# Attention heads of a hybrid decoder layer: the spatial result fetched in turned 32 by 32 blocks and transposed by VectorE instead of TensorE

## The chip, the cores and the metric

The kernel runs on one core of a Trainium2 chip. A core has five engines that run their own queues of instructions: TensorE (PE; its weight loads, which overlap its products, are shown apart as PEld), VectorE (DVE), ScalarE (ACT), GpSimd (POOL) and SyncE (SP), which here issues nearly all transfers. Sixteen DMA engines move data between device memory (HBM) and the on-chip memory SBUF. TensorE writes its results to PSUM, a small memory of eight banks of 128 partitions by 512 floats; the other engines read them there.

The metric is the device time of one launch in microseconds (us). The kernel before takes 1564.72 us, the median of three runs (1563.97 to 1565.47).

## The reference, cut to what matters

One layer with two token mixers, sequence 512, width 2048, sixteen heads and sixteen groups of 128 channels, everything in float32:

```python
proj = h @ w_in[l]
q_lat, kv_lat, k_rope, z_mla, u, v, z_sgu, g_mla, g_sgu = split_cols(proj, IN_SPLITS)
...
y_mla = causal_mla_attention(q_nope, q_rope, k_nope, k_rope, v_mla) * jax.nn.silu(z_mla)
y_sgu = chunked_causal_sgu(u, v, sgu_norm_g[l], w_spatial[l], b_spatial[l]) * jax.nn.silu(z_sgu)
merged = jax.nn.sigmoid(g_mla) * y_mla + jax.nn.sigmoid(g_sgu) * y_sgu
x = x + gate[:, None] * (merged @ w_out[l])
return rmsnorm(x, final_norm_g)
```

What the change touches is the second term of `merged`, sigmoid(g_sgu) * y_sgu, called the spatial result below. For each head (128 channels) it is added to the gated output of the attention.

## The kernel before, in words

Products are made with float32 values split into a high and a low part: three matrix products (`mm3`, lines 148 to 150) for one. The splitting is ScalarE's (a copy to the rounded type, the high part, L118 for weights and L153 for activations) and VectorE's (the difference, the low part, L119 and L136).

The kernel first makes the wide projection, the gates and the spatial result, token blocks by channels, and stores the spatial result in device memory (`t_d`, one tensor for four heads, shape token block x 128 tokens x 512 channels). The gate of the attention's output goes the same way (`gt_d`, for heads 12 to 15 already turned in `g_d`). Then come the sixteen heads, and then the output projection.

In the heads, the merged result is wanted with channels on the partitions and tokens along the row, since it is the left operand of the output projection. The spatial result comes the other way, so it has to be transposed: 128x128 for each of the four token blocks. For head h:

- `scores`: 20 products of the head's queries and keys, one PSUM bank or part of one for each query block; the rotated part of the queries enters by L1560 and L1561.
- `softmax`: VectorE adds the mask and takes the maximum, ScalarE takes the exponentials (L1582), VectorE the reciprocals.
- Meanwhile TensorE makes the queries of head h + 1 (`qproj`), and in even heads also the rotary queries of the next pair (`rproj`).
- `transposes` (L1600): TensorE transposes the exponentials, ScalarE and VectorE split them.
- `kproj`: keys of head h + 1, split by `kfinish` (the row d<-ps,d of L136 on VectorE).
- `turn` (L1626): four TensorE transposes of the gate for heads below 12 (called gated here), and four of the spatial result for all heads.
- `pv`: the product of the transposed exponentials and the values, 12 products into one bank.
- `merge_a`: VectorE multiplies that bank by the gate (sig<-ps,sig, or sig<-ps,g in the last four heads) and adds the transposed spatial result (sig<-sig,ps); the split of the sum is put off to the next head.
- In even heads VectorE then works at two or three pieces of a sum for the output gate (L139); in odd heads it rotates the queries of the next pair (`rfinish`), and TensorE makes the next pair's values (`vproj`).

The program is written in the order in which each engine works; there is no planner in this part. Weights come through `Stream`: a ring of three raw buffers filled by the SP queue (L99) and split by ScalarE and VectorE into a ring of two pairs. The SP queue works in order; a load of weights there waits until VectorE has split the buffer's former contents. `load_before(granule, f)` puts other transfers into that queue just ahead of the load of one granule. The granules of a head are `gq[h]` (queries), `gr[p]` (rotary queries of pair p), `gk[h]` (keys) and `gvv[p]` (values). PSUM banks are handed out in turn from a ring of seven (`bank()`; bank 0 is `rproj`'s).

`fetch(h)` brings the spatial result of a head (tile b, `vt[h]`) and its gate (tile g, `gt[h]`) into SBUF. For heads 1 to 15 it stands ahead of the load of `gk[h]`; head 0's is issued before the first product of the heads.

Of the kernel before, what the change touches and what calls it, by code (L numbers as in the profile page):

```python
# [11 lines left out]
F32 = mybir.dt.float32  # L12
# [8 lines left out]
P = 128  # L21
D = 2048
S = 512
KC = D // P
NB = S // P
# [103 lines left out]
def trunk_layer(ctx, tc, xT, xn, c, vecs, pos, wada, w1, w2, wv, wv3, wv4, wh, wh15, wq, wqr, wk, wvv, wo, wsT, bsp, gfin, out,  # L129
                dbg=None):  # L130
    nc = tc.nc
    ACT, DVE, PE, DMA = nc.scalar, nc.vector, nc.tensor, nc.sync
# [14 lines left out]
    def mm3(ps, ah, al, bh, bl, start, stop):  # L147
        PE.matmul(ps, ah, bh, start=start, stop=False)  # L148
        PE.matmul(ps, ah, bl, start=False, stop=False)  # L149
        PE.matmul(ps, al, bh, start=False, stop=stop)  # L150
# [18 lines left out]
    def nt(p, shape, dt, tag, **kw):  # L169
        uid[0] += 1  # L170
        return p.tile(shape, dt, tag=tag, name=f"{tag}_{uid[0]}", **kw)
# [48 lines left out]
    def scratch(name, shape):  # L220
        return dram.tile(shape, F32, name=name, tag=name)
# [14 lines left out]
    t_d = [scratch(f"t_d{i}", [NB, P, S]) for i in range(4)]  # L236
# [30 lines left out]
    gq, gr, gk, gvv = {}, {}, {}, {}  # L267
# [45 lines left out]
    def get(i, ahead=1, run=1):  # L313
        r = ws.get(i, ahead)
        fs, pend[:] = pend[:run], pend[run:]
        for f in fs:
            f()
        return r
# [8 lines left out]
    def bank_at(k):  # L327
        return nt(psp.p, [P, S], F32, f"ps{k}")

    def bank():  # L330
        n_bank[0] += 1
        return bank_at(ring[(n_bank[0] - 1) % len(ring)])
# [40 lines left out]
    def load_before(granule, f, *a):  # L373
        ws.before.setdefault(granule, []).append(lambda: f(*a))
# [338 lines left out]
    def place(s, us, f, *a):  # L713

        def full(s):
            own, (a, b) = busy.get(s, 0.0) + us, (busy.get(s + d, 0.0) for d in (-1, 1))
            near = [sum(busy.get(s + d + k, 0.0) for k in range(5)) for d in range(-4, 1)]
            return own > 3.3 or own + max(a, b) > 5.75 or s < at_block[T0] + 22 and max(near) + us > 13.4

        while full(s):  # L720
            s += 1
        spend(s, us)
        on(s, BACK, f, *a)
        return s
# [40 lines left out]
    rows = {}  # L765
# [101 lines left out]
    for b in range(1, len(BLOCKS)):  # L867
# [11 lines left out]
        for key in (bl, br_, al, ar):  # L879
            if key[0] == "v":  # L880
                for t in range(2):
                    n, o = 2 * key[2] + t, key[1] * S
# [87 lines left out]
    for g in range(H):  # L970
# [3 lines left out]
        a = s_ + 4  # L974
        on(a, BACK, sgu_scale)
        a = place(a, 0.29, sgu_weights)
        a = place(a, 0.29, sgu_weights_split)
        if g + 1 < H:
            on(a + 1, LOAD, sgu_load, g + 1)
        a = place(max(a, s_ + 5), 0.69, sgu_gain)  # L980
        a = place(a + 1, 0.69, sgu_split)
# [233 lines left out]
    for group in (((10, "lat8"), (11, "lat9")), ((12, "lat10"), ("plain", "sinT"))):  # L1215
# [9 lines left out]
        i = group[0][0]  # L1225
# [124 lines left out]
    bp = tp = None  # L1350
    y_of, z_of = [(1, 2), (0, 7)], (3, 4)
    for b in range(len(BLOCKS)):
        if b == 1:
            ring[:], n_bank[0] = [5, 6], 0
        for g, (p, i) in enumerate(V7):
            s = done[0] = at_block[b] + g
            n = 1 if b or g else 2
# [49 lines left out]
    def at(name, dt, shape=(P, S)):  # L1407
        p, tag = place[name]
        if p is latp.p:
            v = slot(tag, dt)  # L1410
            return v if len(shape) == 2 else v.rearrange("p (n w) -> p n w", n=shape[1])
        return nt(p, list(shape), dt, tag)
# [13 lines left out]
    gt, vt = [None] * H, [None] * H  # L1426
# [34 lines left out]

    def fetch(h):

        vt[h] = nt(bp.p, [P, S], F32, f"b{h}")
        DMA.dma_start(vt[h].rearrange("p (n w) -> p n w", n=NB),
                      t_d[h // 4][:, :, h % 4 * P:(h % 4 + 1) * P].rearrange("n p w -> p n w"))
        gt[h] = nt((ga if h < 8 else g2p).p, [P, S], F32, f"g{h}")
        if h < GATED:
            DMA.dma_start(gt[h].rearrange("p (n w) -> p n w", n=NB),
                          gt_d[h // 4][:, :, h % 4 * P:(h % 4 + 1) * P].rearrange("n p w -> p n w"))  # L1470
        else:
            DMA.dma_start(gt[h], g_d[h - GATED])

    for h in range(1, H):
        load_before(gk[h], fetch, h)


    qt, kt, vv, qs = {}, {}, {}, {}

    def qproj(h, meanwhile=None, then=None):  # L1480
        wH, wL = get(gq[h])
        if meanwhile:
            meanwhile()
        ps = bank()
        for k in range(6):
            sl = slice(k * P, (k + 1) * P)
            mm3(ps, wH[:, sl], wL[:, sl], lh[k], ll[k], k == 0, k == 5)
        if then:
            then()
        qh, ql = at("qh", F32R), at("ql", F32R)  # L1490
        hilo(qh, ql, ps)
        qt[h] = (qh, ql)

    def rproj(p):
        wH, wL = get(gr[p])
        ps = bank_at(0)
        for k in range(6):
            sl = slice(k * P, (k + 1) * P)
            mm3(ps, wH[:, sl], wL[:, sl], lh[k], ll[k], k == 0, k == 5)
        return ps  # L1500
# [12 lines left out]
    def kproj(h):  # L1513
        wH, wL = get(gk[h])
        ps = bank()
        for k in range(4):
            sl = slice(k * P, (k + 1) * P)
            mm3(ps, wH[:, sl], wL[:, sl], lh[6 + k], ll[6 + k], k == 0, k == 3)
        return ps
# [28 lines left out]
    def scores(h):  # L1548
        qh, ql = qt.pop(h)
        kh, kl = kt.pop(h)  # L1550
        q2 = qs.pop(h)
        s3, s2, s1 = bank(), bank(), bank()
        dst = {3: s3, 2: s2[:, :384], 1: s1[:, :256], 0: s1[:, 256:384]}
        for i in (3, 2, 1, 0):
            ps = dst[i]
            n = (i + 1) * P
            q = slice(i * P, (i + 1) * P)
            mm3(ps, qh[:, q], ql[:, q], kh[:, :n], kl[:, :n], True, False)

            PE.matmul(ps, q2[:, q], krh[:, :n], start=False, stop=False)  # L1560
            PE.matmul(ps, q2[:, q], krl[:, :n], start=False, stop=True)  # L1561
        return dst
# [59 lines left out]
    def turn(src):  # L1622
        ps = bank()
        for n in range(NB):
            tk = slice(n * P, (n + 1) * P)
            PE.transpose(ps[:, tk], src[:, tk], ident)  # L1626
        return ps
# [13 lines left out]
    def merge(n=None):  # L1641
        fs, merging[:] = merging[:n], merging[n:] if n else []
        for f in fs:
            f()

    merging = []
    fetch(0)
    rps = rproj(0)
    m2 = at("m2", F32)
    qproj(0, lambda: [f() for f in last_gates], lambda: ws.split_to(gvv[0]))  # L1650
# [7 lines left out]
    def out_granule(cg, i, banks, ahead=1, run=1):  # L1658
        wH, wL = get(go[cg, i], ahead, run)
        for k in range(2):  # L1660
            j = 2 * i + k
            sl = slice(k * 512, (k + 1) * 512)
            for n in range(NB):
                tk = slice(n * P, (n + 1) * P)
                mm3(banks[n], mh[j][:, tk], ml[j][:, tk], wH[:, sl], wL[:, sl], j == 0, j == H - 1)

    for h in range(H):
        if h == H - 1:
            ring[:], n_bank[0] = [4, 5, 6, 7], 0
            ws.split_to(go[0, 0])  # L1670
        dst = scores(h)
        more, odd = h + 1 < H, h % 2 == 1
        pair = h // 2 + 1
        first = go[0, 1] if not more else gr[pair] if not odd and 2 * pair < H else None
        pr_, shares_ = softmax(h, dst, (lambda: ws.split_to(first)) if first is not None else None)
        if more:
            qproj(h + 1, lambda: merge(1 if h == H - 2 else None))
            if not odd and 2 * pair < H:
                rps = rproj(pair)
        else:  # L1680
            pso = [bank_at(k) for k in range(NB)]
            for i in range(2):
                out_granule(0, i, pso)
        pa, fa = transposes(pr_, (0,))
        fa()
        if h < GATED:
            for n in range(NB):
                g_ = gt[h][:, n * P:(n + 1) * P]
                ACT.activation(g_, g_, AF.Copy, scale=shares_[:, n:n + 1])
        pb, fb = transposes(pr_, (1,))  # L1690
        fb()
        pc, fc = transposes(pr_, (2, 3))
        fc()
        if more:
            kps = kproj(h + 1)
            kfinish(h + 1, kps)
        else:
            merge()
            pieces_at(h)
            DVE.tensor_reduce(out=dots[:, 2 * KC:2 * KC + NG], in_=partial, axis=AX.X, op=ALU.add)  # L1700
            gate_sum(0, NG)
            out_granule(0, 2, pso)
            gate_turn(0, NG, bank(), nt(tp, [P, S], F32, "sig", bufs=3))()
        gate_ = gt[h]
        if h < GATED:
            gate_ = nt(tp, [P, S], F32, "sig", bufs=3)
            ACT.copy(gate_, turn(gt[h]))
        tps = turn(vt[h])
        ops = pv(h, {**pa, **pb, **pc})
        merge_a(h, ops, tps, gate_)  # L1710
        if not odd:
            pieces_at(h)
        if not odd and 2 * pair < H:
            m2 = at("m2", F32)
            swapped(m2, rps)
        if more and odd:
            rfinish(pair, rps, m2)
            vproj(pair)
# [36 lines left out]
    rows = []  # L1755
# [39 lines left out]
    for cg in range(3):  # L1795
# [6 lines left out]
        for n in range(NB):  # L1802
            f = lambda n=n, cg=cg, ps=pso[n]: residual(n, cg, slice(cg * 512, (cg + 1) * 512), ps)
# [7 lines left out]
    for n in range(NB):  # L1811
# [16 lines left out]
        y, o = yt[:, n], 1536 + o  # L1828
# [82 lines left out]
```

## Time and profile before

| | |
|---|---|
| median of three runs | 1564.72 us |
| the profiled execution | 1566.76 us, span of its instructions 1565.1 us |
| granted clock of TensorE, mean | 0.999 |
| busy over the span: TensorE, its weight loads, VectorE, ScalarE | 99%, 83%, 78%, 51% |
| DMA | 316.16 MB, 202 GB/s on average |
| heads | from about 1097 to 1400 us |
| L1626 on tile b | 64 transposes, 272 ns each from start to end |
| fetch of tile b | 16 transfers of 256 KB, median 4.9 us from issue to landing |

Times in the profile are microseconds from the start of the span. A row of a group gives line, engine, operation, what is written and read, shape, count, then busy time, mean ns of one, and idle time just before with what ended it. A row of a timeline gives start, duration, engine and work. An engine's idle time costs something only where the end of the kernel depends on it.

### The profile page before, as it was taken

What the parts mean: (1) busy time and instruction counts of PE and PEld (TensorE: products, weight loads), DVE (VectorE), ACT (ScalarE), POOL (GpSimd) and SP (SyncE); (2) the same over time, 40 slices, a digit from 0 to 9 for tenths busy, and PEclk for the clock granted to TensorE, in tenths of its full rate; (3) what the DMA queues carried; (4) which work ended last, traced back from release to release, by engine and by line L of the source; (5) the groups of instructions that cost most, each with busy time, mean ns of one, the idle gap of its engine ahead of it and who ended that gap; (6) DMA issues with size and microseconds to landing.
All of it is one profiled execution on the core that took longest, in us unless ns stands there. A gap on an engine that the chain in (4) does not pass through costs nothing.

```text
span 1565.1 us, 20574 instructions
## 1 busy us (share of the span) xinstructions
PE 1552.7 (99%) x7392; PEld 1296.2 (83%) x7392; DVE 1218.7 (78%) x1667; ACT 802.9 (51%) x1238; POOL 70.5 (5%) x67
## 2 busy tenths in 40 slices
PE   9999999999999999999999999999999999999998
PEld 7888778888888888888888888888888888888887
DVE  8989777778787879787879797878777777865753
ACT  4445555546545555545555565647655555532332
POOL 0000000101010101020100010100000000000000
PEclk9999999999999999999999999999999999999999
DMA  9979565858785877786867685967443433348722
GB/s 377 376 273 353 163 190 162 240 138 243 231 234 171 233 216 214 210 227 192 224 183 204 203 253 160 258 164 223 142 122 122 127 112 118 96 133 333 262 88 108
DMA packets 237224, 316.16 MB, mean 202 GB/s; under 512 B 16201, under 2 KB 184193, under 8 KB 231489
## 3 DMA queue, kind: packets, MB, share of 16 engines
q1 hardware_dynamic: 214210, 291.78, 57.0%
q0 software_dynamic: 22912, 23.07, 9.6%
q8 instruction: 58, 0.95, 0.2%
q14 instruction: 44, 0.36, 0.1%
HBM read 291.11 MB, written 23.68 MB: 201 GB/s over the span
## 4 chain that ended last, share of the span: by engine, by line
PE 91%; DMA 3%; DVE 3%; ACT 1%; issue 1%; SPq 0%; DVEq 0%; ACTq 0%
PE ps L1384 16%; PE ps L1386 16%; PE ps L1385 16%; PE ps L149 12%; PE ps L150 12%; PE ps L148 12%; PE ps L443 5%; DMA X<-in_wh 2%; PE ps L1600 1%; PE ps L1626 1%; DMA wraw<-in_w 1%; PE ps L1560 1%; PE ps L1561 1%; DVE X L136 1%; DVE d L136 0%
## 5 line engine op out<-in xcount | busy, mean ns | idle before, releaser
L136 DVE TENSOR_TENSOR X<-X,X 128x1024 fp32r<-128x1024 f32 (+2 forms) x111 | 130.5, 1182 | 32.7 <-ACT X L629 31.1
L629 ACT CAST X<-X 128x1024 fp32r<-128x1024 f32 x70 | 73.6, 1052 | 100.0 <-PE ps L1385 54.4
L629 ACT CAST w0h<-X 128x1024 fp32r<-128x1024 f32 x70 | 73.7, 1052 | 97.7 <-PE ps L1385 54.3
L629 ACT CAST w1h<-X 128x1024 fp32r<-128x1024 f32 x69 | 72.6, 1052 | 79.3 <-PE ps L1385 43.7
L136 DVE TENSOR_TENSOR w0l<-X,w0h 128x1024 fp32r<-128x1024 f32 x70 | 85.5, 1221 | 28.1 <-ACT w0h L629 27.9
L136 DVE TENSOR_TENSOR w1l<-X,w1h 128x1024 fp32r<-128x1024 f32 x69 | 84.3, 1221 | 24.7 <-ACT w1h L629 23.6
L119 DVE TENSOR_TENSOR w0l<-wraw,w0h 128x1024 fp32r<-128x1024 f32 (+4 forms) x61 | 64.3, 1053 | 40.4 <-ACT w0h L118 37.9
L118 ACT CAST w0h<-wraw 128x1024 fp32r<-128x1024 f32 (+4 forms) x61 | 56.0, 918 | 75.2 <-PE ps L150 21.1
L118 ACT CAST w1h<-wraw 128x1024 fp32r<-128x1024 f32 (+4 forms) x60 | 50.5, 841 | 83.7 <-PE ps L150 21.9
L136 DVE TENSOR_TENSOR X<-wraw,X 128x1024 f32<-128x1024 f32 (+1 forms) x65 | 79.3, 1221 | 17.2 <-ACT X L629 15.0
L1386 PE MATMUL ps<-w1l,hh 128*128 128x512 f32 x236 | 91.9, 390 | 0.2 <-DVE w1l L136 0.2
L1384 PE MATMUL ps<-w1h,hh 128*128 128x512 f32 x236 | 91.9, 389 | 0.0
L1385 PE MATMUL ps<-w1h,hl 128*128 128x512 f32 x236 | 91.9, 389 | 0.0
L1385 PE MATMUL ps<-w0h,hl 128*128 128x512 f32 x236 | 91.8, 389 | 0.0
L1384 PE MATMUL ps<-w0h,hh 128*128 128x512 f32 x236 | 91.8, 389 | 0.0
L1386 PE MATMUL ps<-w0l,hh 128*128 128x512 f32 x236 | 91.8, 389 | 0.0
L1386 PE MATMUL ps<-X,hh 128*128 128x512 f32 x232 | 90.6, 391 | 0.2 <-DVE X L136 0.2
L1384 PE MATMUL ps<-X,hh 128*128 128x512 f32 x232 | 90.4, 390 | 0.0
L1385 PE MATMUL ps<-X,hl 128*128 128x512 f32 x232 | 90.3, 389 | 0.0
L139 DVE SCALAR_TENSOR_TENSOR wada<-wada,cact 128x2048 f32<-128x2048 f32 x39 | 88.9, 2282 | 0.6 <-DMA wada<-in_wada 0.6
L119 DVE TENSOR_TENSOR w1l<-wraw,w1h 128x1024 fp32r<-128x1024 f32 (+4 forms) x60 | 57.4, 957 | 33.6 <-ACT w1h L118 32.7
L148 PE MATMUL ps<-hh,w1h 128*128 128x512 f32 x204 | 81.3, 399 | 0.0
(410 smaller groups left out, 4418.3 us busy)
## 6 DMA issues: line engine op xcount, KB each, us to landing
X<-in_wh SPq DMA_DIRECT2D x131, 512.0 KB, 5.0
wada<-in_wada SPq DMA_DIRECT2D x39, 1024.0 KB, 7.4
wraw<-in_wo SPq DMA_DIRECT2D x32, 512.0 KB, 4.2
wraw<-in_wh SPq DMA_DIRECT2D x21, 512.0 KB, 4.7
wraw<-in_wh POOLq DMA_DIRECT2D x21, 512.0 KB, 7.9
X<-in_wv SPq DMA_DIRECT2D x17, 512.0 KB, 3.7
X<-in_wh SPq DMA_DIRECT2D x22, 384.0 KB, 5.2
wraw<-in_w SPq DMA_DIRECT2D x16, 512.0 KB, 9.5
```

The costliest lines, as they stand in the source:

```text
L118: self.nc.scalar.copy(hi[:, :n], raw[:, :n])
L119: self.nc.vector.tensor_tensor(out=lo[:, :n], in0=raw[:, :n], in1=hi[:, :n].bitcast(F32), op=ALU.subtract)
L136: DVE.tensor_tensor(out=out, in0=in0, in1=in1, op=op)
L139: DVE.scalar_tensor_tensor(out=out, in0=in0, scalar=scalar, in1=in1, op0=op0, op1=op1, **kw)
L148: PE.matmul(ps, ah, bh, start=start, stop=False)
L149: PE.matmul(ps, ah, bl, start=False, stop=False)
L150: PE.matmul(ps, al, bh, start=False, stop=stop)
L443: PE.matmul(ps1[m], a[:, cols[m]], b, start=(j == 0 and a is wH and b is hh[j]), stop=False)
L629: ACT.copy(hi, t)
L1384: PE.matmul(ps[t].rearrange("p (h w) -> p h w", h=4), xh[:, tk], wH[:, k], start=st, stop=False, skip_group_check=True)
L1385: PE.matmul(ps[t].rearrange("p (h w) -> p h w", h=4), xl[:, tk], wH[:, k], start=False, stop=False, skip_group_check=True)
L1386: PE.matmul(ps[t].rearrange("p (h w) -> p h w", h=4), xh[:, tk], wL[:, k], start=False, stop=sp, skip_group_check=True)
```

## The change

The spatial result is no longer fetched by `fetch`, but by a new function `fetch_blocks`, in four transfers a head, one for each 32 channels. Each fills 32 partitions: in partition i, for each of the 16 token blocks of 32 tokens, the 32 channels (128 bytes) of token i of that block. So every 32 by 32 block lies where its transposed block belongs, and only the blocks themselves are still to be turned. One instruction of VectorE (`DVE.transpose`, 128x512, in place) turns all 64 blocks of a head. It stands where the four TensorE transposes stood, and the merge adds the tile in SBUF instead of the PSUM bank. `fetch_blocks(h)` stands ahead of the load of `gq[h]`, which comes before `gk[h]`; head 0's follows `fetch(0)`. The gate's transposes are not changed.

```diff
@@ fetch
-        vt[h] = nt(bp.p, [P, S], F32, f"b{h}")
-        DMA.dma_start(vt[h].rearrange("p (n w) -> p n w", n=NB),
-                      t_d[h // 4][:, :, h % 4 * P:(h % 4 + 1) * P].rearrange("n p w -> p n w"))
         gt[h] = nt((ga if h < 8 else g2p).p, [P, S], F32, f"g{h}")
...
+    SQ = 32
+
+    def fetch_blocks(h):
+
+        vt[h] = nt(bp.p, [P, S], F32, f"b{h}")
+        rows = t_d[h // 4].rearrange("n (a i) w -> i (n a) w", i=SQ)
+        for b in range(P // SQ):
+            o = h % 4 * P + b * SQ
+            DMA.dma_start(vt[h][b * SQ:(b + 1) * SQ].rearrange("i (m j) -> i m j", j=SQ), rows[:, :, o:o + SQ])
+
     for h in range(1, H):
         load_before(gk[h], fetch, h)
+        load_before(gq[h], fetch_blocks, h)
...
     fetch(0)
+    fetch_blocks(0)
     rps = rproj(0)
...
             ACT.copy(gate_, turn(gt[h]))
-        tps = turn(vt[h])
+        DVE.transpose(out=vt[h], in_=vt[h])
+        tps = vt[h]
         ops = pv(h, {**pa, **pb, **pc})
```

On VectorE, at the end of head 0, there stood (kfinish's split, then the two passes of the merge, then the pieces):

```order
L119 TENSOR_TENSOR w0l_9182<-wraw_55_8996,w0h_9181 128x768
L136 TENSOR_TENSOR d_1384_8978<-ps_1412_9187,d_1384_8978 128x512
L136 TENSOR_TENSOR sig_9227<-ps_1416_9214,sig_9202 128x512
L136 TENSOR_TENSOR sig_9227<-sig_9227,ps_1415_9209 128x512
L139 SCALAR_TENSOR_TENSOR piece_8951,dots_93<-piece_8951,cq_8949 128x512
```

and now stands:

```order
L119 TENSOR_TENSOR w0l_9191<-wraw_55_9007,w0h_9190 128x768
L136 TENSOR_TENSOR d_1384_8984<-ps_1413_9201,d_1384_8984 128x512
L1717 STREAM_TRANSPOSE b_1371_8885<-b_1371_8885 128x512
L136 TENSOR_TENSOR sig_9237<-ps_1416_9224,sig_9216 128x512
L136 TENSOR_TENSOR sig_9237<-sig_9237,b_1371_8885 128x512
L139 SCALAR_TENSOR_TENSOR piece_8959,dots_93<-piece_8959,cq_8957 128x512
```

The transpose has moved in between the split of the keys and the merge, and the merge's second pass reads b.

On the SP queue, where the heads begin (wvv is the load of the first pair's values, wq and wqr those of head 1's queries and the next pair's rotary queries), there stood:

```order
L99 DMA wraw_51_8854<-in_wvv 128x1024
L1465 DMA b_1370_8883<-t_d_144 128x4x128
L1469 DMA g_1371_8885<-gt_d_141 128x4x128
L99 DMA wraw_52_8887<-in_wq 128x768
L99 DMA wraw_53_8913<-in_wqr 128x768
```

and now stands:

```order
L99 DMA wraw_51_8854<-in_wvv 128x1024
L1466 DMA g_1370_8883<-gt_d_141 128x4x128
L1479 DMA b_1371_8885<-t_d_144 32x16x32 x4
L1479 DMA b_1372_8890<-t_d_144 32x16x32 x4
L99 DMA wraw_52_8895<-in_wq 128x768
L99 DMA wraw_53_8921<-in_wqr 128x768
```

Head 1's four transfers have come in ahead of wq, beside head 0's. Later in the loop four transfers stand ahead of each wq, and g alone ahead of wk.

## The prediction

> **What bounds the kernel now.** I read the page's busy shares and its chain first, then the stretches of the sixteen heads (about 1097 to 1400 us), then who waits there.
>
> ```profile
> span 1565.1 us, 20574 instructions
> PE 1552.7 (99%) x7392; PEld 1296.2 (83%) x7392; DVE 1218.7 (78%) x1667; ACT 802.9 (51%) x1238; POOL 70.5 (5%) x67
> PE 91%; DMA 3%; DVE 3%; ACT 1%; issue 1%; SPq 0%; DVEq 0%; ACTq 0%
> ```
>
> Two stretches of 40 us (columns: length, then busy time of TensorE, its weight loads, VectorE, ScalarE, GpSimd; granted clock, DMA share, GB/s), and the waits of TensorE's weight loads from 1100 to 1400 (us in total, times, longest):
>
> ```profile
> 1100.00:1140.00 40.00, 40.00 (x237) 35.35 (x236) 30.44 (x67) 24.61 (x62) 0.00 (x0) 1.00 0.42 125
> 1340.00:1380.00 40.00, 39.20 (x235) 34.45 (x234) 34.30 (x78) 17.27 (x39) 0.00 (x0) 1.00 0.32 100
> ```
>
> ```profile
> PEld ps L1600 <- ACT hl L1582: 2.1, 6, 0.3
> PEld ps L1600 <- DVE hl L143: 1.0, 1, 1.0
> ```
>
> TensorE (PE) is busy all the time, carries 91% of the chain, and in the stretches it is full or nearly so at clock 1.00, while VectorE (DVE) works 30 to 34 us and the DMA engines 32 to 42%. TensorE's waits here are small: 2.1 us in six odd heads and 1.0 us in head 13, always before the softmax transposes of L1600. So time taken out of TensorE's row shows in the end, unless VectorE, which gets new work, or a load becomes late.
>
> **What is removed.** Four transposes a head, 64 in all. What one set costs in the row of work is the distance between starts of weight loads: from the first transpose of b to the first load of the product with v.
>
> ```profile
> 1110.91 0.47 PEld L1626 LDWEIGHTS ps<-ident,b 128*128 128x128 f32 x4
> 1111.35 0.19 PEld L148 LDWEIGHTS ps<-hh,d 128*128 128x128 f32 x1
> ...
> 1337.59 0.58 PEld L1626 LDWEIGHTS ps<-ident,b 128*128 128x128 f32 x4
> 1338.15 0.19 PEld L148 LDWEIGHTS ps<-hh,d 128*128 128x128 f32 x1
> ```
>
> (Timelines here and below: start, duration, then engine and work, and in brackets idle time before it and what ended that.) Head 0: 1111.35 - 1110.91 = 0.44 us. Head 12, with no gate transposes ahead: 1338.15 - 1337.59 = 0.56. Heads 0 to 11 and 15 go by the first, 12 to 14 by the second: 13 x 0.44 + 3 x 0.56 = 7.4 us off TensorE. A taking of a PSUM bank goes with them, so the ring of seven turns sooner: the bank of head 0's keys, read by VectorE at 1111.50, is now taken again by head 1's first softmax transposes at 1120.75 (rows below), and the others of the ring by like work; 8 us of cover, no cost.
>
> **What is added on VectorE.** One 128x512 block transpose a head, in place. The add behind it reads SBUF instead of PSUM. No row shows this transpose, so its cost is bounded by other 128x512 float rows:
>
> ```profile
> L143 DVE TENSOR_SCALAR y<-y,ry 128x512 f32<-128x512 f32 x8 | 3.5, 484 | 0.1
> L136 DVE TENSOR_TENSOR g<-sig,b 128x512 fp32r<-128x512 f32 x16 | 10.9, 684 | 0.7 <-ACT b L153 0.7
> L136 DVE TENSOR_TENSOR w0l<-X,w0h 128x1024 fp32r<-128x1024 f32 x70 | 85.5, 1221 | 28.1 <-ACT w0h L629 27.9
> L139 DVE SCALAR_TENSOR_TENSOR wada<-wada,cact 128x2048 f32<-128x2048 f32 x39 | 88.9, 2282 | 0.6 <-DMA wada<-in_wada 0.6
> ```
>
> Nearest is a plain pass over 512 elements a partition, 0.68 us; I take 0.7. The low end is 0.48; the high end, if blocks had to be read several times over, 2.28, that of 2048 elements. The merge's add is 0.69 from PSUM (1114.32 below), a pass that reads SBUF alone 0.68: no change. Whether 0.7 us matters is decided by VectorE's idle time at that place, between the split of the next head's keys and the merge, which waits for the product with v:
>
> ```profile
> 1111.50 0.68 DVE L136 TENSOR_TENSOR d<-ps,d 128x512 fp32r<-128x512 f32 x1
> 1113.59 0.69 DVE L136 TENSOR_TENSOR sig<-ps,sig 128x512 f32<-128x512 f32 x1 [1.41 <-PE ps L150]
> 1114.32 0.69 DVE L136 TENSOR_TENSOR sig<-sig,ps 128x512 f32<-128x512 f32 x1
> 1114.92 0.69 DVE L139 SCALAR_TENSOR_TENSOR piece<-piece,cq 128x512 f32<-128x512 f32 x1
> ...
> 1126.74 0.68 DVE L136 TENSOR_TENSOR d<-ps,d 128x512 fp32r<-128x512 f32 x1
> 1127.69 0.69 DVE L136 TENSOR_TENSOR sig<-ps,sig 128x512 f32<-128x512 f32 x1 [0.27 <-PE ps L150]
> ...
> 1131.72 0.69 DVE L136 TENSOR_TENSOR hl<-hh,hl 64x512 fp32r<-64x512 f32 x1 [0.69 <-ACT hl L1507]
> ...
> 1133.22 0.96 DVE L119 TENSOR_TENSOR w1l<-wraw,w1h 128x768 fp32r<-128x768 f32 x1
> 1134.59 0.30 DVE L136 TENSOR_TENSOR ps<-ps,mask 128x128 f32<-128x128 f32 x1 [0.41 <-PE ps L1561]
> ...
> 1138.74 0.96 DVE L119 TENSOR_TENSOR w0l<-wraw,w0h 128x768 fp32r<-128x768 f32 x1 [0.48 <-ACT w0h L118]
> ...
> 1340.33 0.69 DVE L136 TENSOR_TENSOR sig<-ps,g 128x512 f32<-128x512 f32 x1 [1.00 <-PE ps L150]
> ...
> 1354.63 0.69 DVE L136 TENSOR_TENSOR sig<-ps,g 128x512 f32<-128x512 f32 x1 [0.93 <-PE ps L150]
> ...
> 1361.60 0.30 DVE L136 TENSOR_TENSOR ps<-ps,mask 128x128 f32<-128x128 f32 x1 [0.48 <-PE ps L1561]
> ```
>
> And the weight loads of TensorE that take what VectorE makes there:
>
> ```profile
> 1120.75 0.20 PEld L1600 LDWEIGHTS ps<-ident,hl 128*128 128x128 f32 x2 [0.35 <-ACT hl L1582]
> ...
> 1133.70 0.19 PEld L1560 LDWEIGHTS ps<-hh,hl 128*128 128x128 f32 x1
> ...
> 1140.77 0.19 PEld L150 LDWEIGHTS ps<-hh,w0l 128*128 128x128 f32 x1
> ```
>
> Even gated heads (the row at 1113.59): idle 1.41. The product ends 0.44 sooner, so 0.97 is left, and 0.7 fits. This matters, because the chain from here is tight: merge, two pieces, mask and maximum, exponentials, and then TensorE waits for it in the next (odd) head (1120.75, idle 0.35). It starts 0.44 sooner and ends 0.44 sooner, so the odd head's wait stays as long as it was and the gain passes through.
>
> Odd gated heads (1127.69): idle 0.27. With the product 0.44 sooner and the transpose in front, VectorE is 0.7 + 0.44 - 0.27 = 0.9 us late against TensorE. Next in line is the rotation of the queries: L1560 takes its result (hl) at 1133.70, and it is done at 1131.72 + 0.69 = 1132.41, 1.3 us of cover. Then the weight split, done at 1134.18, 0.41 us of idle before the mask: there VectorE is still 0.9 - 0.41 = 0.5 late. Then the split that the second projection needs, done at 1139.70 and wanted at 1140.77: 1.07 us of cover. The softmax transposes of these even heads come only after that projection, without a wait in the row of waits. Cost: nothing.
>
> Heads 12 and 14: idle 1.00, less 0.56, less 0.7: 0.26 us late. Part of that is not lost, since the idle time is counted from the end of the row ahead while a pass can start 0.1 us before the one ahead of it ends (1114.32 and 1114.92: 0.60 apart, 0.69 long). I take 0.1 each, 0.2 us of loss together. Head 13 (idle 0.93 at 1354.63) is 0.3 late, which head 14's idle of 0.48 ahead of its mask (1361.60) covers.
>
> **The transfers.** One fetch of 512 pieces of 512 B becomes four of 512 pieces of 128 B each, and it is moved ahead of the loading of wq instead of wk; head 1's now stands with head 0's before the first wq of the loop, eight transfers where one of b stood (the rows of the SP queue stand with the change).
>
> Four views: a stretch in which only fetches of b and g run, issues on the SP queue, the landing of wq, and ScalarE's first use of two of these loads.
>
> ```profile
> 1136.75:1138.50 1.75, 1.75 (x10) 1.42 (x9) 1.37 (x6) 1.75 (x5) 0.00 (x0) 1.00 1.10 333
> ```
>
> ```profile
> 1050.31 3.97 SPq L1259 DMA_DIRECT2D sinT<-rope_d  x4
> ...
> 1080.71 0.35 SPq L99 DMA_DIRECT2D wraw<-in_wq  x1
> ...
> 1097.65 0.35 SPq L99 DMA_DIRECT2D wraw<-in_wq  x1
> ...
> 1105.50 0.34 SPq L99 DMA_DIRECT2D wraw<-in_wvv  x1
> 1111.61 0.33 SPq L99 DMA_DIRECT2D wraw<-in_wq  x1
> ```
>
> ```profile
> wraw<-in_wq SPq DMA_DIRECT2D x16, 384.0 KB, 3.1
> ```
>
> ```profile
> 1095.81 0.83 ACT L118 CAST w1h<-wraw 128x768 fp32r<-128x768 f32 x1
> ...
> 1109.74 0.85 ACT L118 CAST w0h<-wraw 128x768 fp32r<-128x768 f32 x1
> ```
>
> In the first row the fetches of head 4 (b and g, 1024 pieces) fill the DMA engines for 1.75 us, 1.7 ns a piece. By bytes a head's b still costs 0.9 us; by pieces 2048 x 1.7 = 3.5 us. At the dear end the load of the DMA engines rises by 2 x 2.6 us in 40, from 0.42 to 0.55. Issue: the nearest four of such a 32-partition shape took 3.97 us, 1.0 each. In the loop SP sits waiting for VectorE between wvv (1105.50) and wq (1111.61), so four issues are hidden, and wq issued at 1097.65 is first used at 1109.74, 12 us later. At the start, eight issues of 1.0 move the wq of 1080.71 to about 1088, and 3.1 us later, or at the dear end's 7 us of pieces from 1080 no later than that, it has landed by about 1092; ScalarE takes it at 1095.81. Hidden, with 4 us to spare. The tiles themselves are wanted later than the weights behind them: head 0's, fetched from 1080 on, after 1111.50.
>
> A rule that speaks against this: the Trainium skill ("DMA: Bandwidth & Descriptors", Specifications) says that below 512 B a DMA engine does read-modify-write. No row here isolates 128 B pieces. If by that a piece cost twice the dear end, the eight fetches would last 14 us from 1080, the first wq would land about 1 us late, and the sum would be 1 us worse.
>
> **Sum.** 7.4 gained, 0.2 lost: 7.2 us. The profiled execution took 1566.76 us (span 1565.1), which is 2.0 above the median of the runs, 1564.72; the change is taken off the median: 1557.5 us.
>
> **Rivals.**
> *Partly given back.* The transpose takes as long as a pass over 1024 elements, 1.22 us. Even gated heads are then 1.22 - 0.97 = 0.25 late, six times; heads 12 and 14 0.78 each (1.22 + 0.56 - 1.00); the six odd ones about 0.1 at the queries (1.39 late against 1.3); head 14's mask 0.4 (head 13's 1.22 + 0.56 - 0.93 = 0.85 against 0.48): 1.5 + 1.6 + 0.6 + 0.4 = 4.1 lost, 3.3 gained, 1561.4. For it: no row shows the operation, and blocks are read one way and written the other. Against it: the passes over 512 elements above take 0.48 to 0.69 whatever they do. The Trainium skill ("VectorE: DVE Perf Modes", The three transpose paths) gives 311 ns for 128 columns of bf16; four such would be 1.24, an estimate and close to this rival, but one instruction needs its fixed part only once.
> *Slower: VectorE's transpose becomes the bound.* From 1.22 us on, the covers are used up in some 15 heads, so each tenth of a microsecond costs 1.5 us; the gain is gone at 1.22 + 3.3/15 = 1.44 us. At the high end, 2.28 us, it is 15 x 1.06 - 3.3 = 12.6 us worse than before: 1577. TensorE would then wait before L1600 in every odd head.
> *The loads become late.* 128 B pieces at several times the dear end hold up wq in each head: needs more than 12 us a head, that is over 6 ns a piece against 1.7. At 8 ns, 16 us of transfer against 12 of cover, 4 us a head: 64 us slower. Against it: the load share of 0.42 and the cover above.
> *No gain to speak of.* If the odd heads' wait before L1600 is set by something that doesn't move, the 0.44 is given back in seven heads and 1557.5 becomes 1560.6; if even heads have such a tie too, it stays at 1564.7. Against it: VectorE's rows from the product's end to the mask have no idle time.
>
> **Chances.** As summed, 0.68; partly given back, either way, 0.13; no gain, 0.05; slower by VectorE 0.08, by loads 0.06. About 0.2% (3 us) is what a measurement can tell from no change, so the partly returned case at 1561.4 lies just on its edge: faster 0.79, within 0.2% 0.07, slower 0.14. The range goes from 1555.8 (the low price of the transpose and 1 us for runs that differ by 1.5) to 1563.0, which takes in the partly given back cases and leaves out the slower ones.
>
> **What would show it.** Transposes of VectorE of 0.7 us; no L1626 on b; odd heads' waits before L1600 still about 0.3 us; no wait of L118 for a DMA; from 1100 to 1400 7 us less. Wrong if the transposes are over 1.2 us, or if ScalarE's splits wait for wq.

## The result and the profile after

The changed kernel takes 1558.42 us, the median of five runs (1558.25 to 1559.32), beside 1565.09 us for the kernel before (1563.97 to 1565.48, five runs). The ratio is 0.9956, with a 95% interval of 0.9946 to 0.9967: faster by 6.7 us, or 0.4%. The profiled execution took 1558.25 us.

The page of the changed kernel: span, busy shares, transfers, and the chain that ended last by engine.

```profile
span 1556.5 us, 20498 instructions
PE 1544.6 (99%) x7328; PEld 1289.3 (83%) x7328; DVE 1226.8 (79%) x1683; ACT 802.6 (52%) x1238; POOL 69.6 (4%) x67
DMA packets 262568, 316.15 MB, mean 203 GB/s; under 512 B 49737, under 2 KB 209537, under 8 KB 256833
PE 94%; DVE 2%; DMA 2%; SPq 1%; issue 1%; ACT 1%; DVEq 0%; ACTq 0%
```

TensorE has 64 instructions fewer and 8.1 us less busy time, and it still bounds the kernel. VectorE has 16 instructions more. Nearly the same bytes are moved (316.15 MB against 316.16), in more pieces: 49737 packets are now under 512 B, against 16201 in the kernel before. The spans differ by 8.5 us (1565.06 and 1556.54), though the medians differ by 6.7: the profiled execution before was 1.7 us above its median of five, this one 0.2 below.

The two stretches of the heads (columns as in the prediction):

```profile
1100.00:1140.00 40.00, 40.00 (x233) 35.19 (x232) 32.64 (x68) 24.99 (x61) 0.00 (x0) 1.00 0.47 131
1340.00:1380.00 40.00, 39.11 (x223) 33.80 (x222) 33.83 (x73) 18.14 (x40) 0.00 (x0) 1.00 0.31 95
```

TensorE is as full as before at clock 1.00. In the first stretch VectorE went from 30.44 to 32.64 us and the DMA share from 0.42 to 0.47. The waits of TensorE's weight loads from 1090 to 1400 us (L1608 is the former L1600, L1568 the former L1560):

```profile
PEld ps L1608 <- ACT hl L1590: 2.1, 6, 0.4
PEld ps L1608 <- PE ps L150: 1.1, 1, 1.1
...
PEld ps L1568 <- DVE hl L136: 0.4, 1, 0.4
PEld ps L149 <- DVE w0l L119: 0.3, 1, 0.3
```

They are the old waits at their old sizes: 2.1 us in six odd heads, and one of about 1 us in head 13. The two small ones at the end of the list stood at 0.4 us each in the same stretch before. No wait took the place of the removed work.

VectorE's groups on the new operation and the merge behind it, and its timeline at the ends of heads 0, 1 and 12:

```profile
L1717 DVE STREAM_TRANSPOSE b<-b 128x512 f32<-128x512 f32 x16 | 11.2, 701 | 0.0
L136 DVE TENSOR_TENSOR sig<-ps,sig 128x512 f32<-128x512 f32 x12 | 8.1, 671 | 2.2 <-PE ps L150 2.2
```

```profile
1109.87 0.69 DVE L136 TENSOR_TENSOR d<-ps,d 128x512 fp32r<-128x512 f32 x1
1110.47 0.70 DVE L1717 STREAM_TRANSPOSE b<-b 128x512 f32<-128x512 f32 x1
1111.54 0.69 DVE L136 TENSOR_TENSOR sig<-ps,sig 128x512 f32<-128x512 f32 x1 [0.36 <-PE ps L150]
...
1125.29 0.70 DVE L1717 STREAM_TRANSPOSE b<-b 128x512 f32<-128x512 f32 x1
1125.91 0.65 DVE L136 TENSOR_TENSOR sig<-ps,sig 128x512 f32<-128x512 f32 x1
...
1131.40 0.96 DVE L119 TENSOR_TENSOR w1l<-wraw,w1h 128x768 fp32r<-128x768 f32 x1
1132.28 0.29 DVE L136 TENSOR_TENSOR ps<-ps,mask 128x128 f32<-128x128 f32 x1
...
1332.55 0.70 DVE L1717 STREAM_TRANSPOSE b<-b 128x512 f32<-128x512 f32 x1
1333.18 0.69 DVE L136 TENSOR_TENSOR sig<-ps,g 128x512 f32<-128x512 f32 x1
```

The block transpose takes 0.701 us. In head 0 it fits into the idle time ahead of the merge, with 0.36 us to spare. In head 1 and in head 12 no idle time is left ahead of the merge, and head 1's lateness uses up the idle time ahead of the next mask (1132.28). All of that ends before it reaches TensorE.

The transfers: SP's queue and ScalarE at the start of the heads, and the landing times by group.

```profile
1077.56 6.24 SPq L1479 DMA_DIRECT2D b<-t_d  x8
1083.92 0.41 SPq L99 DMA_DIRECT2D wraw<-in_wq  x1
...
1093.53 0.62 ACT L1516 CAST hh<-hh 64x512 fp32r<-64x512 f32 x1
1094.17 0.83 ACT L118 CAST w1h<-wraw 128x768 fp32r<-128x768 f32 x1
```

```profile
b<-t_d SPq DMA_DIRECT2D x64, 64.0 KB, 3.9
wraw<-in_wq SPq DMA_DIRECT2D x16, 384.0 KB, 3.3
```

Eight issues took 6.24 us, 0.78 each. The wq behind them is issued at 1083.92 and lands some 3.3 us later; ScalarE takes it at 1094.17, straight after its own work (L1516), so it does not wait. In the trace's packets, 128 B take 13.4 ns on average (32768 of them) and 512 B 30.1 ns (27.3 ns for those in the stretch from 1070 to 1400 us).

**Where the time went.** Where each head begins (the first weight load of L1568, L1560 before), minus the same in the profile before:

| head 0 | 1 | 2 | 6 | 12 | 13 | 14 | 15 | end |
|---|---|---|---|---|---|---|---|---|
| -1.63 | -2.06 | -2.51 | -4.17 | -6.71 | -7.15 | -7.55 | -8.01 | -8.52 |

The first 1.63 us are there ahead of the heads: they belong to the profiled execution of before, which was that much above its median. From head 0 to the end 6.89 us are gained, 0.40 to 0.46 in each of the heads 0 to 14 and 0.51 from the start of head 15 to the end. The medians say 6.67.

### The profile page after: what moved, and what is told of

It is laid out like the page before. It is cut to its first block, busy times and chain, and to the rows that moved or that the text cites. A ratio compares the mean times of both kernels' runs of the same rounds, so it can differ in the third digit from the quotient of the medians.

```text
span 1556.5 us, 20498 instructions
## 1 busy us (share of the span) xinstructions
PE 1544.6 (99%) x7328; PEld 1289.3 (83%) x7328; DVE 1226.8 (79%) x1683; ACT 802.6 (52%) x1238; POOL 69.6 (4%) x67
## 2 busy tenths in 40 slices
DMA packets 262568, 316.15 MB, mean 203 GB/s; under 512 B 49737, under 2 KB 209537, under 8 KB 256833
## 4 chain that ended last, share of the span: by engine, by line
PE 94%; DVE 2%; DMA 2%; SPq 1%; issue 1%; ACT 1%; DVEq 0%; ACTq 0%
PE ps L1384 17%; PE ps L1386 17%; PE ps L1385 17%; PE ps L149 12%; PE ps L150 12%; PE ps L148 12%; PE ps L443 5%; PE ps L1608 1%; PE ps L1568 1%; DMA wraw<-in_w 1%; PE ps L1569 1%; DVE d L136 0%; PE ps L1634 0%; SPq L1479 0%; DMA lat<-v_d 0%
## 5 line engine op out<-in xcount | busy, mean ns | idle before, releaser
L139 DVE SCALAR_TENSOR_TENSOR wada<-wada,cact 128x2048 f32<-128x2048 f32 x39 | 88.9, 2282 | 0.4 <-DMA wada<-in_wada 0.4
```

The source lines that it names most:

```text
L139: DVE.scalar_tensor_tensor(out=out, in0=in0, scalar=scalar, in1=in1, op0=op0, op1=op1, **kw)
```

## The experiments

The first four ask what the removed work was worth and how near VectorE is to its limit, the next three ask about the transfers, and the rest about the wait that stayed. "Before" has its own median in each series: 1565.3 us with the first four, 1565.6 with the next four, 1565.3 with the last four.

### No transposition on any engine

```diff
-        DVE.transpose(out=vt[h], in_=vt[h])
         tps = vt[h]
```

and the fetch of the kernel before.

> As the changed kernel, but the spatial result is fetched in the old way and turned by no engine (left out: its transposition; it is added as it lies). Theory (TensorE's four transposes were the price, VectorE's transpose and the small pieces are hidden): 1558.2 us, within 0.8 of the changed kernel, and heads that pass 0.43 us sooner each than in the kernel before. Heads 12 and 14 may gain up to 0.1 each, since VectorE's 0.70 us is gone there. Rival (the transpose or the fetch eats a part of the gain): faster than the changed kernel by over 1 us, at most by the 7.4 us that the prediction took for the four transposes, less 6.7: 0.7 in the heads, the rest elsewhere.

Measured: 1558.50 us (1558.21 to 1559.11), the changed kernel's time. VectorE has its idle time back:

```profile
L136 DVE TENSOR_TENSOR sig<-ps,sig 128x512 f32<-128x512 f32 x12 | 8.2, 686 | 5.9 <-PE ps L150 5.9
```

5.9 us of idle time ahead of the merge against 2.2, and nothing comes of it. Heads 12, 13 and 14 gain 0.43, 0.40 and 0.47 us here, as against 0.44, 0.40 and 0.46 with the transpose. So VectorE's work and the new fetch together cost nothing that these runs can tell.

### TensorE's four transposes put back beside VectorE's

```diff
+        turn(vt[h])
         DVE.transpose(out=vt[h], in_=vt[h])
```

> The changed kernel with TensorE's four transposes of the spatial result put back beside VectorE's, into a bank that nobody reads. Theory: the time of the kernel before, 1565.1 us, within 0.8: 64 transposes at some 0.11 us are all the gain. Rival (part of the gain is from the fetch's new place, or from the merge that reads SBUF in place of PSUM): it stays at least 1 us under the kernel before. Rival (VectorE's transpose has a cost that the gain covered): over the kernel before by more than 1 us.

Measured: 1565.29 us (1564.95 to 1566.16), ratio to before 1.0001 (0.9991 to 1.0010). The whole gain is gone, and its head starts move by no more than 0.05 us against those of before from head 0 to head 15. So all of the gain is the 64 transposes: 1565.29 - 1558.42 = 6.9 us, 0.43 a head (against the kernel without any transposition, which ran beside it, 6.8). The weight loads of this run, with both sets of four in one head:

```profile
1108.80 0.59 PEld L1634 LDWEIGHTS ps<-ident,g 128*128 128x128 f32 x4
1109.36 0.47 PEld L1634 LDWEIGHTS ps<-ident,b 128*128 128x128 f32 x4
1109.80 0.19 PEld L148 LDWEIGHTS ps<-hh,d 128*128 128x128 f32 x1
```

The set that stands behind a product (the gate's) is 0.56 us long by this view, the set behind it 0.44.

### The block transpose twice, and three times

```diff
         DVE.transpose(out=vt[h], in_=vt[h])
+        DVE.transpose(out=vt[h], in_=vt[h])
```

> The changed kernel with the block transpose done twice (so the blocks are turned back; the transposition within the blocks is left out). It prices VectorE's margin: 0.70 us more a head, 1.40 in all. Prediction's steps, with its covers: even gated heads have 0.97 us of idle left, so 0.43 late, six times: 2.6; heads 12 and 14 0.6 each: 1.2; the queries of the odd heads (cover 1.3 us, now some 1.6 late): 0.3, six times: 1.8. Sum about +5, 1563 to 1564 us. Rival (VectorE has more slack than I counted): +1 or less, 1559. Rival (VectorE is already the bound): the whole 0.70 in 15 heads, +10.5, 1569.

> The changed kernel with the block transpose done three times (result as with one). Prediction's slope: beyond the margin each 0.1 us costs 0.1 in about 15 heads, so 10.5 us over the kernel with two: about 1574 us, and TensorE waits for VectorE's or ScalarE's work of the softmax (L1610) in the odd heads and for the queries (L1570) after them. Rival (only the even heads are tied): half of it, 1568. Rival (slack remains): under 1562.

Measured: 1562.02 us with two (1560.78 to 1562.53; 0.9978 of before, 0.9969 to 0.9987), 1573.57 with three (1573.29 to 1574.48; 1.0053, 1.0038 to 1.0068). TensorE's waits with two, and then with three:

```profile
PEld ps L1608 <- ACT hl L1590: 3.7, 6, 0.6
PEld ps L1568 <- DVE hl L136: 1.9, 7, 0.4
PEld ps L1608 <- issue: 1.8, 1, 1.8
PEld ps L149 <- DVE w0l L119: 1.1, 1, 1.1
```

```profile
PEld ps L1608 <- ACT hl L1590: 8.2, 6, 1.4
PEld ps L1568 <- DVE hl L136: 6.6, 8, 1.0
```

The waits grow at the two places expected: before the softmax transposes of the odd heads, and at the queries. The expectation for three was right. For two it was 1 to 2 us too dear. A second transpose starts 0.74 us after the first (in the run with three, they start at 1110.37, 1111.11 and 1111.85). The second costs 3.6 us in all, the third 11.55, which is 0.74 us in 15.6 heads: from there on each tenth of a microsecond costs 1.6 us. Between the two the gain is gone: 1562.02 and (1565.3 - 1562.02)/15.6 = 0.21 us more, so a block transpose of about 0.70 + 0.74 + 0.21 = 1.65 us would have been worth nothing. That is an estimate on the line between the two runs; no run has such a transpose.

### The old fetch with VectorE's transpose

```diff
@@ fetch
+        vt[h] = nt(bp.p, [P, S], F32, f"b{h}")
+        DMA.dma_start(vt[h].rearrange("p (n w) -> p n w", n=NB),
+                      t_d[h // 4][:, :, h % 4 * P:(h % 4 + 1) * P].rearrange("n p w -> p n w"))
...
-        load_before(gq[h], fetch_blocks, h)
...
-    fetch_blocks(0)
```

> The changed kernel with the old fetch: one transfer a head of 512 B pieces, ahead of the load of wk (the 32 by 32 blocks then lie in the wrong places, so the exchange of blocks is left out; VectorE's transpose stays). Theory (the four transfers, their 128 B pieces and their place are hidden): 1558.4 us, within 0.8 of the changed kernel. Rival (small pieces or four issues hold up weights): faster than the changed kernel by 1 us or more.

Measured: 1558.22 us (1558.00 to 1558.83), the same. Neither the small pieces nor the four issues cost anything that these runs can tell.

### Smaller pieces and more issues

```diff
-            DMA.dma_start(vt[h][b * SQ:(b + 1) * SQ].rearrange("i (m j) -> i m j", j=SQ), rows[:, :, o:o + SQ])
+            for e in range(0, SQ, 16):
+                DMA.dma_start(vt[h][b * SQ:(b + 1) * SQ].rearrange("i (m j) -> i m j", j=SQ)[:, :, e:e + 16],
+                              rows[:, :, o + e:o + e + 16])
```

(for 64 B pieces; for 32 B four steps of 8 channels).

> The changed kernel with each of its four transfers a head cut in two (16 of the 32 channels each): eight issues and 64 B pieces. Issues lie some 0.8 us apart in the changed kernel where the first eight stand. Sixteen of them move the first wq from 1083.9 to about 1090.3 us; 3.3 us to landing gives 1093.6 or, with twice the pieces, up to 1096, and ScalarE takes it at 1094.2: 0 to 2 us late once. Later heads: eight issues of 0.8 us in a head of 14.3 us, hidden. Sum 1558.5 to 1560.5 us. Rival (the queue is already tight, or pieces below 128 B are rewritten at twice the price): weights late in each head, over 1565 us. Rival (issues overlap wholly): 1558.4.

> The changed kernel with each of its four transfers a head cut in four (8 of the 32 channels each): sixteen issues and 32 B pieces. Thirty-two issues of 0.8 us at the start move the first wq to about 1103 us and its landing to 1106, 12 us after ScalarE's use at 1094.2: about 12 us lost once. In the loop 16 x 0.8 = 13 us of issues a head and 8192 pieces at 10 ns on sixteen DMA engines, 5 us, against a head of 14.3 us: the queue is nearly full, some us lost in each head: 1570 to 1600 us. Rival (an issue costs a fraction of 0.8 us where nothing holds the queue): under 1562.

Measured: 1558.56 us with eight issues a head (1557.48 to 1559.08), still hidden, and 1572.39 with sixteen (1570.96 to 1572.66; 1.0042 of before, 1.0029 to 1.0056). With sixteen, SP's queue and ScalarE at the start, and TensorE's first product after its wait:

```profile
1077.82 19.41 SPq L1480 DMA_DIRECT2D b<-t_d  x32
1097.33 0.43 SPq L99 DMA_DIRECT2D wraw<-in_wq  x1
...
1101.27 0.83 ACT L118 CAST w1h<-wraw 128x768 fp32r<-128x768 f32 x1 [6.87 <-DMA wraw<-in_wq]
```

```profile
1102.16 0.80 PE L148 MATMUL ps<-hh,w1h 128*128 128x512 f32 x1 [4.92 <-ACT w1h L118]
1102.75 0.63 PE L149 MATMUL ps<-hl,w1h 128*128 128x512 f32 x1
```

Thirty-two issues took 19.4 us, so the first wq goes out at 1097.33 and ScalarE waits 6.87 us for it. Head 1 begins 12.0 us later relative to before than head 0 does, and head 2 another 1.1. After that each head gains its 0.43 us as in the changed kernel. So the first half of the expectation held (some 12 us lost once). Its second half, a queue too full in every head, did not: it took a head for 14.3 us long, while heads 0 to 11 begin 17.5 and 19.4 us apart in turn, and behind the start sixteen issues took 12.1, 10.5 and 9.4 us. The measured 1572.39 lies in the expected range all the same, by the loss at the start alone, and that is luck. What broke was the row of issues ahead of the first wq, not the price of the pieces: 32 B took 8.8 ns, 64 B 10.8 and 128 B 13.4.

### VectorE's pieces of the output gate's sum moved ahead

The wait that stayed before L1608 of the odd heads is the end of a chain: merge, pieces (L139), mask and maximum, exponentials. In even heads VectorE has idle time (2.50 us in head 0) ahead of the splits of its softmax transposes, and the pieces don't depend on the merge.

```diff
+        if not odd and h < H - 2:
+            pieces_at(h)
         pa, fa = transposes(pr_, (0,))
...
         merge_a(h, ops, tps, gate_)
-        if not odd:
+        if h == H - 2:
             pieces_at(h)
```

> The changed kernel with VectorE's pieces of the output gate's sum (L139) of the even heads 0 to 12 moved from behind the merge to ahead of the transposes of the same head's exponentials, where VectorE is idle. That takes some 1.2 us out of the chain from the product with v through the pieces, mask and exponentials to the next odd head's softmax transposes (L1608). Theory (that chain is what TensorE waits for there): the six waits of 0.35 us and the one of 1.1 us in head 13 go: 2.1 + 1.1 = 3.2, so 1555.2 us. Rival (the wait is tied to the exponentials by something else): 1558.4. Rival (the pieces collide with ScalarE's scaling or the splits in the middle of the head): slower than 1559.

Measured: 1556.75 us (1556.12 to 1557.45), faster than the changed kernel, but by 1.7 us and not by 3.2. Both kernels ran again on one chip, since the difference is small:

> The changed kernel, unchanged, beside the next one on the same chip: 1558.4 us, within 0.8.

> The kernel with the pieces moved ahead, unchanged, beside the changed kernel on the same chip. Theory (the six waits of TensorE's weight loads in the odd heads cost 0.14 us each, by the starts of the heads, and head 13's 1.0: 1.8 in all): 1.3 to 2.1 us below the changed kernel. Rival (the difference of 1.7 between two separate series is drift): within 0.5 of it.

Measured: 1558.39 us (1557.92 to 1560.13) for the changed kernel, 1556.61 (1555.53 to 1557.86) with the pieces ahead. No run of the one reaches into the runs of the other; against before the ratio is 0.9945 (0.9932 to 0.9959). The waits of the repeated run with the pieces ahead:

```profile
PEld ps L1608 <- PE ps L1608: 0.6, 2, 0.3
PEld ps L1568 <- DVE hl L136: 0.4, 1, 0.4
PEld ps L149 <- DVE w0l L119: 0.3, 1, 0.3
```

All seven waits are gone, 3.2 us by the view of waits, and yet only 1.7 us is gained. The weight loads of head 1 show why, first in the changed kernel, then with the pieces ahead:

```profile
1118.16 0.19 PEld L150 LDWEIGHTS ps<-hh,w0l 128*128 128x128 f32 x1
1118.70 0.21 PEld L1608 LDWEIGHTS ps<-ident,hl 128*128 128x128 f32 x2 [0.35 <-ACT hl L1590]
1118.87 0.25 PEld L1608 LDWEIGHTS ps<-ident,d 128*128 128x128 f32 x2
```

```profile
1118.40 0.19 PEld L150 LDWEIGHTS ps<-hh,w0l 128*128 128x128 f32 x1
1118.63 0.38 PEld L1608 LDWEIGHTS ps<-ident,hl 128*128 128x128 f32 x2
1118.97 0.14 PEld L1608 LDWEIGHTS ps<-ident,d 128*128 128x128 f32 x1
```

From the last load of the projection to the loads of d it is 0.71 us with the wait and 0.57 without: a wait of 0.35 costs 0.14. The weight loads run ahead of the products (the load of the gate's first transpose starts at 1108.80 in the run with both sets, its product at 1109.03), and the two loads on hl, which start at once without the wait, then take 0.34 to the next instead of 0.17. Six times 0.14, and 0.87 in head 13 (1.27 us gained there against before, where the changed kernel gained 0.40), make 1.7. By the starts of the heads it is 0.11 to 0.15 in each of the six.

### Pieces ahead, and the block transpose twice

> The pieces moved ahead and the block transpose done twice (transposition within the blocks left out). It asks which cover the second transpose exceeds. The kernel with two transposes lost 3.6 us, its rows of waits showing 3.7 us before L1608 in the six odd heads, 1.8 in head 13 and 1.9 at the queries' product (L1568). Theory (the loss lies in the chain merge, pieces, mask, exponentials that the even heads hand to the odd ones, and at the queries): moving the pieces ahead gives that chain 1.2 us, so only the queries' waits of about 0.3 us in seven heads stay, and 0.5 in head 14, where nothing moved: 1556.75 + 2.1 + 0.5, about 1559.3 us. Rival (VectorE's total work is the limit): it keeps its 3.6 us over the kernel with one transpose: 1560.4.

Measured: 1557.77 us (1557.62 to 1558.12), 1.2 us over the same kernel with one transpose, where two had cost 3.6 us without the move. That is below both expectations. The waits at the queries did not stay:

```profile
PEld ps L149 <- DVE w0l L119: 1.0, 1, 1.0
PEld ps L1608 <- PE ps L1608: 0.8, 2, 0.5
PEld ps L1608 <- PE ps L150: 0.5, 1, 0.5
PEld ps L1568 <- DVE hl L136: 0.4, 1, 0.4
```

L1568 waits once again. The lateness of the odd heads' queries had been handed on from the even heads before them: the merge of head 1 starts 14.1 us after the head's first load here, and 15.2 us after it with two transposes and no move. What is left lies at the end of the row of heads: 0.5 us before L1608 in head 13, and 1.0 for a split of weights (w0l) in head 15, behind head 14, whose pieces were not moved. VectorE's total is not what limits; the chain through the even heads' ends is.

### The four transfers ahead of wk

```diff
+        load_before(gk[h], fetch_blocks, h)
         load_before(gk[h], fetch, h)
-        load_before(gq[h], fetch_blocks, h)
...
-    fetch(0)
     fetch_blocks(0)
+    fetch(0)
```

> The changed kernel with its four transfers ahead of the load of wk in place of wq, and head 0's ahead of its gate's. Theory (the place in the queue is hidden): 1558.4 us, within 0.8. Four issues now lie before each wk, which is issued at 1101.06 in the changed kernel and used some 14 us later, so 3 us of delay are covered. Rival (wk is late by them): over 1560.

Measured: 1557.91 us (1557.77 to 1558.56), 0.5 us below the changed kernel of the same series (1557.92 to 1560.13) and within the 0.8 expected. The place is hidden.

## Why the prediction was right, point by point

The forecast was 1557.5 us in a range of 1555.8 to 1563.0; it is 1558.42, 0.9 above, and the forecast's side and mechanism held. The gain is 6.7 us where 7.2 was summed: 0.5 of the 0.9. The other 0.4 is the median that the sum was taken off, 1564.72 of three runs, where five give 1565.09.

- **What bounds.** TensorE, right: it is 99% busy before and after, and time taken out of its row showed in the end. Its list of TensorE's waits was not complete: the same view also holds 0.6 us between transposes of L1600 and 0.4 us before L149 for a split of weights. Both stayed as they were, so nothing hung on them.
- **What is removed.** The 0.44 us a head was right to 0.02: heads 0 to 11 gain 6.71 - 1.63 = 5.08 us, 0.42 each, against 12 x 0.44 = 5.28. The step that was mis-sized is "Heads 0 to 11 and 15 go by the first, 12 to 14 by the second", with 0.56 for the second: measured are 0.44, 0.40 and 0.46, 1.30 us in place of 1.68. The 0.56 was read as a distance of weight loads behind a product, and those run ahead of the products; the run with both sets shows 0.56 for whichever set stands first and 0.44 for the next. By the products head 12's set cost 0.44 too: from the start of the last product ahead of it to that of the second product behind it, it was 1338.49 - 1337.59 = 0.90 us before, and is 1331.35 - 1330.89 = 0.46 now.
- **The 0.2 us of loss** in heads 12 and 14 did not come: without any transpose those heads gain the same to 0.01 us. Of the three heads together 1.68 - 0.2 = 1.48 us was expected, and 1.30 came: two errors that partly cancel, which is luck.
- **The block transpose.** Taken at 0.7 from the nearest rows, 0.701 measured. The high bound of 2.28, and the estimate of 1.24 from the bf16 figure of the Trainium skill ("VectorE: DVE Perf Modes", The three transpose paths), were far off for one instruction of four such tiles.
- **Its covers.** Even gated heads: 0.27 us of idle time should have been left, 0.36 is. Odd gated heads: late as worked out, the idle time ahead of the mask is used up, and L1568 waits no longer than before. The odd heads' wait before L1608 stays at 2.1 us, so the gain passed through as the prediction argued.
- **The transfers.** 0.78 us an issue in place of 1.0, so the first wq went out at 1083.92, not 1088 (1086.4 in this profile, which runs 1.6 us ahead of the one before), and had some 7 us to spare rather than 4. A piece's 13.4 ns on one of sixteen engines make 2048 x 13.4/16 = 1.7 us a head, between the bounds of 0.9 and 3.5. The rule that below 512 B a DMA engine does read-modify-write (the Trainium skill, "DMA: Bandwidth & Descriptors", Specifications) would have cost 1 us if it doubled the dear end. Here a 128 B packet took 13.4 ns against 30.1 for 512 B, dearer by the byte and cheaper by the piece, and the old fetch gave the same time.
- **The rivals.** "Partly given back" and "slower" had the right places and nearly the right slope (1.5 us for each 0.1 us; 1.6 measured from the second to the third transpose), but the point at which the gain is gone was too near: 1.44 us, where the runs give about 1.65. With two transposes in a row, 0.70 + 0.74 = 1.44 us, 3.3 us of the gain was still there. Part of the reason is that the covers hold more than was worked out: the even gated heads would be 1.44 - 0.97 = 0.47 us late. In the run with two the merge starts 0.63 us after the second transpose does (1111.48 and 1112.11 in head 0), before that one has ended. So it starts 0.74 + 0.63 = 1.37 us after the first one, where the product allows 1111.54 - 1110.47 = 1.07: 0.30 late, and the wait before L1608 grew by (3.7 - 2.1)/6 = 0.27. Another part is that a wait of weight loads is dearer in the view than in time: the view has 4.8 us more of them with two transposes than with one (9.3 against 4.5), and 3.6 us was lost. What makes up the rest stays open. "Loads late" was sought in the price of the pieces; the runs found it in the issues at the start, at four times as many. "No gain" is refuted by the steady 0.43 us a head.
- **The PSUM ring.** No cost was seen, and with the bank taken again beside the new work the time was that of before. It was not tried alone.

## What to carry to other kernels

Where TensorE was full and another engine had a gap at the right place, moving work off TensorE gained TensorE's time, 0.43 us a head, and nothing was lost elsewhere. What has to be worked out is not the other engine's total but the chain behind the gap: which pass comes next, and how much cover each has. Prices for removed work should be taken from products or from the second of two like sets, since a distance or a wait of weight loads behind a product contains time in which TensorE still works. And where a chain is tight, look for work in it that doesn't depend on its head: the two or three pieces of another sum, moved ahead, gave 1.7 us for a few lines, and the fastest version of all.

## What the runs showed of the hardware that was not expected

A wait that the view of waits puts at 0.35 us cost 0.14; 3.2 us of such waits were worth 1.7.

Consecutive block transposes in place on one tile start 0.74 us apart, and the two passes of the merge, of which the second reads what the first wrote, 0.69 to 0.73 apart. Passes of the same length that don't depend on each other start 0.60 to 0.64 apart.

When TensorE stood still for 4.92 us in the run with sixteen issues a head, the next products took 0.80 and 0.63 us, where the same form takes 0.40 on average. It stood still once more, for 3.23 us up to 1122.74, and the next product again took 0.80 us. The granted clock (the last figure but two) in stretches of that run:

```profile
1094.00:1100.50 6.50, 3.24 (x20) 2.62 (x18) 1.16 (x2) 0.40 (x1) 0.00 (x0) 1.00 0.64 79
1101.00:1107.50 6.50, 5.34 (x12) 4.01 (x13) 4.58 (x13) 4.55 (x10) 0.00 (x0) 0.50 1.03 381
1108.00:1121.00 13.00, 11.50 (x62) 9.66 (x60) 4.58 (x9) 4.62 (x11) 0.00 (x0) 1.00 0.63 100
1121.50:1128.00 6.50, 4.95 (x14) 4.06 (x15) 5.70 (x12) 3.97 (x7) 0.00 (x0) 0.50 0.78 138
1128.50:1138.00 9.50, 9.50 (x53) 8.02 (x53) 7.61 (x20) 8.09 (x21) 0.00 (x0) 1.00 0.83 222
```

Each time the clock falls to one half while TensorE stands still, stays there for at least 6.5 us, and is full again by 1108.0 and 1128.5. The Trainium skill ("TensorE: Matmul & The Clock Gate", Part 1) says that TensorE drops to half its clock after an idle window of some 3.4 us. The trace agrees in the half, and the second pause, 3.23 us by the view, is a little shorter than that.

So late loads cost more than the waits they make. Against the changed kernel head 1 begins 12.4 us later (the 12.0 against before, and the 0.43 that head 0 gains in the changed kernel). The two pauses are 4.92 + 3.23 = 8.15 us of it. At half the clock the twelve products from 1102.16 to 1107.58 took 5.42 us, where twelve of them 0.23 us apart, as they are at full clock, would take 2.76; the three from 1122.74 to 1124.87 took 2.13 in place of 0.69. That is 4.1 us more, some short waits for splits (0.49 and 0.31 us) among it, and 12.25 in all. Head 2's further 1.1 us fall into the rest of the second stretch. This is worked out from the rows; no run changes the clock by itself.
